# Hybrid decoder block: weight passes in another order, phase arithmetic in other pieces, last scaling by four rows

## The chip, the cores and the metric

The program runs on one core of one Trainium2 chip. The metric is the device time of one execution, in microseconds; the shown time of the kernel before is the median of three runs, 2548.59 us (2547.72 to 2549.03).

## The reference

One layer on 512 tokens of 2048 channels, all in float32. A token mixer has two branches from one projection `w_in` (2048 to 8192 columns): a diagonal state-space branch (64 groups of 64 complex states, a scan over 512 tokens, GELU, a gate `w_glu`, then `w_ssm_out`), and a short gated convolution (three taps, `w_conv_out`). Both are merged by sigmoid gates and go through `w_o`. A gated MLP follows (`w_up` to 2 x 5632, a causal three-tap convolution, GELU, `w_down`), with RMSNorm before each part and at the end:

```python
h = h + token_mixer(rmsnorm(h, norm_tok[l]), w_in[l], a_re[l], a_im[l], log_dt[l], ...)
h = h + conv_ffn(rmsnorm(h, norm_ffn[l]), w_up[l], ffn_conv_w[l], ffn_conv_b[l], w_down[l])
return rmsnorm(h, norm_final)

abar_re = mag * jnp.cos(dt * ai); abar_im = mag * jnp.sin(dt * ai)   # in s5_scan
_, _, xr, xi = lax.associative_scan(combine, (a_seq_re, a_seq_im, bu_re, bu_im), axis=1)
yb = (gate_b * causal_dwconv(gate_c * v, conv_w, conv_b)) @ w_conv_out  # in token_mixer
```

## The kernel before

Channels lie on the 128 partitions and the 512 tokens run along the free axis. Every product with a weight is taken in three passes of rounded numbers: weight and activation are each split into a rounded part (hi) and the remainder (lo), and hi·hi, hi·lo and lo·hi are added up in PSUM. A `Unit` is one output tile of 128 channels; it consists of chunks of eight (in `w_down` six) weight tiles of 128x128, and a chunk of eight is 24 matmuls (`products`, lines 156 to 170).

`run` goes through all chunks in order. After the matmuls of chunk i it calls `after(i)` (line 172), which puts the instructions of the other engines into their queues: first the preparation of chunk i+3 (`prep_to`), then loads, then so many pieces from the list `bg` as the unit says, then the unit's hooks, and at a unit's last chunk its `done`. Each engine works through its own queue in this order, so what is written earlier stands earlier. Three buffers each hold the raw weights (`wraw`), hi (`whi`) and lo (`wlo`).

`prep_to` makes hi by a ScalarE copy (L150). Lo is made in one of two ways. In most of the projection `w_in`, for two chunks of three, ScalarE writes the rounded weight with its sign turned into `wlo` (L145) and then hi (L146), and GpSimd issues a DMA that adds the raw weights onto `wlo` (L147). For all other chunks VectorE subtracts hi from the raw weight (L129).

While TensorE works on `w_in`, the state-space branch runs beside it in `bg` pieces, 32 pairs of groups, three pieces to a pair (`bg_pieces`, line 514). `first` issues the complex rotation of an older pair on GpSimd (`ssm_turn`, six instructions) and half a scan on VectorE; `second` the three ScalarE instructions for sine and cosine (`ssm_trig`) and the other half scan; `third` two small matmuls (`ssm_bu`) and the phase of the next pair (`ssm_phase`: on VectorE the outer sum L449, its rounding by adding and subtracting a large number L451, and the difference L452). One scan half is two products that read PSUM (L98), a sum (L478) and the scan (L479).

The 24 units after the eight of the state-space input are eight triples of the convolution branch: `v_done` copies v out of PSUM and multiplies twice by `rstd` on GpSimd, `gc_done` makes the product with gate c (tile `zp`) and at once the three taps (`conv3`: L610 on ScalarE, L611 and L612 on VectorE) and a product on GpSimd, `gb_done` multiplies by gate b. 32 units of merge gates follow, where one chunk issues one piece, and in every fourth unit two.

The up projection of the MLP (`Pair`) has its own order of passes. The down projection is taken in four blocks; in the last one the final four output tiles are done in two halves of 256 tokens (`ends`), so that the norm of the first half can go on while the second is multiplied. `out_store` (line 1170) scales one row of 128 channels by norm and gain per VectorE instruction and stores two rows at a time.

Of the kernel before, what the change touches and what calls it, by code (L numbers as in the profile page):

```python
# [8 lines left out]
F32 = mybir.dt.float32  # L9
# [7 lines left out]
P = 128  # L17
# [33 lines left out]
class Unit:  # L51
# [7 lines left out]
    def __init__(self, chunks, xs, done, pre=None, bg=0, hooks=None, cols=slice(0, T), late=False, post=None):  # L59
        self.chunks, self.xs, self.done, self.pre, self.bg = chunks, xs, done, pre, bg  # L60
        self.hooks, self.cols, self.late, self.post = hooks or {}, cols, late, post
        self.total = sum(c[1] for c in chunks)
        self.k, self.ps = 0, None
        self.acc, self.off = False, 0


# [1 line left out]
def block_kernel(ctx: ExitStack, tc: tile.TileContext, a: dict):  # L68
# [18 lines left out]

    ones = const.tile([P, P], F32, tag="ones", name="ones")
    nc.vector.memset(ones, 1.0)
    halfpi = const.tile([P, 1], F32, tag="halfpi", name="halfpi")  # L90
    nc.vector.memset(halfpi, math.pi / 2)
    warm = const.tile([P, 1], F32, tag="warm", name="warm")
    nc.scalar.activation(warm, halfpi, AF.Copy)
    rstd = const.tile([P, T], F32, tag="rstd", name="rstd")
# [61 lines left out]
    def products(i, j0, j1):  # L156

        u, c = flat[i]
        if u.ps is None:
            u.ps = psm.tile([P, T], F32, tag="mm", name="mm")  # L160
        base = sum(x[1] for x in u.chunks[:c])
        hi, lo = preps[i]
        for j in range(j0, j1):
            xh, xl = (x[:, u.cols] for x in u.xs(base + j))
            w = slice(j * P, (j + 1) * P)
            first, last = u.k == 0, u.k == u.total - 1
            nc.tensor.matmul(u.ps[:, u.cols], hi[:, w], xh, start=first, stop=False)  # L167
            nc.tensor.matmul(u.ps[:, u.cols], hi[:, w], xl, start=False, stop=False)  # L168
            nc.tensor.matmul(u.ps[:, u.cols], lo[:, w], xh, start=False, stop=last)  # L169
            u.k += 1  # L170

    def after(i):

# [78 lines left out]
    def norm_spread(big, cols=slice(0, T)):  # L252
        pb = psm.tile([P, T], F32, tag="mm", name="statb")
        nc.tensor.matmul(pb[:, cols], ones, big[:, cols], start=True, stop=True)
        return pb
# [18 lines left out]
    def st(tag, bufs=1, shape=(P, T), dt=F32):  # L274
        return sp.tile(list(shape), dt, tag=tag, name=tag, bufs=bufs)
# [164 lines left out]
    def ssm_phase(p):  # L440

        br = braw.pop(p)
        bs = st("bst", 3, (P, 2, P), F32R)
        nc.scalar.activation(bs, br, AF.Copy)
        nc.vector.tensor_tensor(bs[64:], br[64:], bs[64:].bitcast(F32), op=ALU.subtract)
        bst[p] = bs
        ph, nk = st("ph", 2), st("nk")
        ph3 = ph.rearrange("p (a b) -> p a b", a=16)
        nc.vector.tensor_tensor(ph3, pha[:, p, :].unsqueeze(2).to_broadcast([P, 16, 32]),  # L449
                                phb[:, p, :].unsqueeze(1).to_broadcast([P, 16, 32]), op=ALU.add)  # L450
        nc.vector.tensor_scalar(nk, ph, MAGIC, MAGIC, op0=ALU.add, op1=ALU.subtract)  # L451
        nc.vector.tensor_tensor(ph, ph, nk, op=ALU.subtract)  # L452
        phs[p] = ph

    def ssm_trig(p):
        ph = phs.pop(p)
        t = pairt("cs", 3)
        nc.scalar.activation(t[:, 1], ph, AF.Sin, scale=TURN)
        nc.scalar.activation(t[:, 0], ph, AF.Abs)
        nc.scalar.activation(t[:, 0], t[:, 0], AF.Sin, scale=-TURN, bias=halfpi)  # L460
        cs[p] = t

    def ssm_bu(p):
        s_, bs = stacks.pop(p), bst.pop(p)
        w = [ph1ps.tile([P, T], F32, tag=f"w{j}", name=f"w{j}") for j in range(2)]
        for j in range(2):
            nc.tensor.matmul(w[j], bs[:, j, :], s_, start=True, stop=True)
        wri[p] = w
# [14 lines left out]
    def ssm_turn(p):  # L483
        t, z = cs.pop(p), zz.pop(p)
        x = pairt("xx", 5)
        for j in range(2):
            w = st("pt")
            mul(x[:, j], z[:, j], t[:, 0], nc.gpsimd)
            mul(w, z[:, 1 - j], t[:, 1], nc.gpsimd)
            nc.gpsimd.tensor_tensor(x[:, j], x[:, j], w, op=ALU.add if j else ALU.subtract)  # L490
        xx[p] = x
# [22 lines left out]
    def bg_pieces(n):  # L514

        def ok(p):
            return 0 <= p < NPAIR

        def quad(m):
            return m % 4 == 3 and ok(m)  # L520

        def first():
            if quad(n - 6):
                ssm_y((n - 6) // 4)
            if quad(n - 5):
                ssm_out((n - 5) // 4)
            if ok(n - 3):
                ssm_turn(n - 3)
            if ok(n - 2):
                ssm_scan(n - 2, 0)  # L530

        def second():
            if ok(n - 1):
                ssm_trig(n - 1)
            if ok(n - 2):
                ssm_scan(n - 2, 1)

        def third():
            if quad(n - 4):
                ur_load((n - 4) // 4)  # L540
            if ok(n - 1):
                ssm_bu(n - 1)
            if ok(n):
                ssm_phase(n)
                ssm_load(n + 1)
        return [first, second, third]
# [43 lines left out]

    def u_first():
        nc.vector.tensor_copy(rstd, norm_spread(big[0]))
        for i in range(4):
            mul(uts[i], uts[i], rstd)

# [18 lines left out]
    def v_done(i):  # L614
        def f(ps):
            hold["v"] = st("mt", 2)
            nc.scalar.activation(hold["v"], ps, AF.Copy)
            mul(hold["v"], hold["v"], rstd, nc.gpsimd)
            mul(hold["v"], hold["v"], rstd, nc.gpsimd)
        return f  # L620

    def gc_done(i):
        def f(ps):
            z = zpad[i % 2]
            mul(z[:, 2:], ps, hold["v"])
            hold["cv"] = st("cv", 2)
            conv3(hold["cv"], z, "cw", "cb", i, KS)
            mul(hold["cv"], hold["cv"], rstd, nc.gpsimd)
        return f

    def gb_done(i):
        def f(ps):
# [17 lines left out]
    for i in range(8):  # L650
        add(Unit(kd_chunks(w_in, 8 + i), xs1, v_done(i), bg=1),
            Unit(kd_chunks(w_in, 24 + i), xs1, gc_done(i), bg=1),
            Unit(kd_chunks(w_in, 16 + i), xs1, gb_done(i), bg=1))
    merges = [Unit(kd_chunks(w_in, 32 + n), xs1, m_done(n), bg=1 + (n % 4 == 0)) for n in range(2 * KD)]
    add(*merges)
    for u, _ in flat[20:]:
# [496 lines left out]
    def dn_done(i, last, cols=slice(0, T)):  # L1153
        def f(ps):
            h = hrow(i, cols)
            nc.vector.tensor_tensor(h, ps[:, cols], h, op=ALU.add)
            if last:
                sumsq(i, cols)
        return f


# [5 lines left out]
    def out_spread(h):  # L1167
        ff["pb"] = norm_spread(ff["big"], HALVES[h])

    def out_store(h, i0, i1):  # L1170
        cols = HALVES[h]
        for i in range(i0, i1):
            x = hrow(i, cols)
            nc.vector.scalar_tensor_tensor(x, x, V("gf", i), ff["pb"][:, cols], op0=ALU.mult, op1=ALU.mult)
            if i % 2:
                x = ff["H"][i // KS][:, i % KS - 1:i % KS + 1, cols]
                (nc.sync if i % 4 == 1 else nc.scalar).dma_start(
                    out[i - 1:i + 1, :, cols].rearrange("a p t -> p a t"), x)

    for b_, (k0, kn) in enumerate(DOWN):  # L1180
        m = 6 if kn == 12 else 8
        last = k0 + kn == KF

        def down(n, **kw):
            return Unit([(a["w_down"][n][:, k * P:(k + m) * P], m) for k in range(k0, k0 + kn, m)],
                        lambda k, k0=k0: xsd(k0 + k), dn_done(n, last, **kw), late=bool(kw), **kw)

        def shifted(u):
            u.off = SHIFT
            return u  # L1190

        dns = [down(n) for n in range(KD - SPLIT if last else KD)]
        if not last:
            k1, n1 = DOWN[b_ + 1]
            if b_ == 0:
                dns[0].hooks[0] = [lambda: [dg_load(k) for k in range(8, 12)]]
            for j in range(n1):
                dns[3 + j].hooks.setdefault(0, []).append(lambda k=k1 + j: dg_split(k))
        add(*map(shifted, dns))
        if last:  # L1200

            ends = [down(n, cols=c) for c in HALVES for n in range(KD - SPLIT, KD)]
            ends[SPLIT].hooks[0] = [lambda: out_sums(0)]
            ends[SPLIT + 1].hooks[0] = [lambda: out_spread(0)]
            ends[SPLIT + 1].post = lambda: out_store(0, 0, 4)
            ends[SPLIT + 2].post = lambda: out_store(0, 4, 8)
            add(*map(shifted, ends))

    run(3, len(flat))

    out_sums(1)
    out_store(0, 8, KD)
    out_spread(1)
    out_store(1, 0, KD)


# [61 lines left out]
```

## Time and profile before

| what | value |
|---|---|
| median of three runs | 2548.59 us |
| the profiled execution | 2549.99 us, of it 2548.2 us span |
| PE busy | 2497.5 us (98%) |
| DVE, ACT, POOL busy | 1711.2, 1048.8, 559.5 us |
| granted TensorE clock, mean over the span | 0.991 |

The profile is of one execution. Times of instructions are counted from the start of its span. PE is TensorE, PEld its weight loads, DVE is VectorE, ACT is ScalarE, POOL is GpSimd, SP the engine that issues most DMAs. Matmuls overlap one another, so that their durations add up to more than the time they take; the pace is read from counts in a stretch. An idle time is put down to what ended it.

### The profile page before, as it was taken

What the parts mean: (1) busy time and instruction counts of PE and PEld (TensorE: products, weight loads), DVE (VectorE), ACT (ScalarE), POOL (GpSimd) and SP (SyncE); (2) the same over time, 40 slices, a digit from 0 to 9 for tenths busy, and PEclk for the clock granted to TensorE, in tenths of its full rate; (3) what the DMA queues carried; (4) which work ended last, traced back from release to release, by engine and by line L of the source; (5) the groups of instructions that cost most, each with busy time, mean ns of one, the idle gap of its engine ahead of it and who ended that gap; (6) DMA issues with size and microseconds to landing.
All of it is one profiled execution on the core that took longest, in us unless ns stands there. A gap on an engine that the chain in (4) does not pass through costs nothing.

```text
span 2548.2 us, 36443 instructions
## 1 busy us (share of the span) xinstructions
PE 2497.5 (98%) x14616; PEld 2195.8 (86%) x14616; DVE 1711.2 (67%) x1979; ACT 1048.8 (41%) x1331; POOL 559.5 (22%) x431
## 2 busy tenths in 40 slices
PE   8999999999999999999999999999999999999997
PEld 7877777777888888888999999999999988888887
DVE  7799999999323555446777777888787753333335
ACT  5344444444233433334455455555555532222222
POOL 1067767687202121110000000000000000000011
PEclk9999999999999999999999999999999999999999
DMA  5766677777445334444666666676666673434335
GB/s 186 224 165 174 172 187 188 188 190 194 144 147 203 120 132 141 145 142 128 169 174 185 175 167 170 192 190 181 166 177 183 188 254 109 132 108 130 99 94 152
DMA packets 149337, 418.40 MB, mean 164 GB/s; under 512 B 17840, under 2 KB 26160, under 8 KB 149168
## 3 DMA queue, kind: packets, MB, share of 16 engines
q1 hardware_dynamic: 121648, 330.88, 40.8%
q0 software_dynamic: 20448, 74.46, 15.5%
q10 hardware_dynamic: 7072, 10.74, 1.2%
q8 instruction: 114, 1.87, 0.3%
q14 instruction: 55, 0.45, 0.1%
HBM read 300.67 MB, written 40.89 MB: 134 GB/s over the span
## 4 chain that ended last, share of the span: by engine, by line
PE 80%; DMA 5%; DVE 5%; issue 4%; POOL 3%; ACT 2%; SPq 0%; ACTq 0%; DVEq 0%; POOLq 0%
PE mm L169 18%; PE mm L167 18%; PE mm L168 18%; PE sr L1029 9%; PE sr L1027 8%; PE sr L1028 8%; DMA wlo<-wraw 2%; DVE wlo L129 2%; ACT whi L150 1%; DMA wraw<-wraw 1%; POOL pt L98 1%; POOL xx L98 1%; POOL xx L490 1%; PE py L498 1%; DMA th<-ghl 0%
## 5 line engine op out<-in xcount | busy, mean ns | idle before, releaser
L129 DVE TENSOR_TENSOR wlo<-wraw,whi 128x1024 fp32r<-128x1024 f32 (+1 forms) x396 | 479.7, 1211 | 368.8 <-ACT whi L150 368.3
L150 ACT ACTIVATE whi<-wraw 128x1024 fp32r<-128x1024 f32 (+1 forms) x396 | 395.3, 999 | 488.4 <-PE mm L168 391.5
L169 PE MATMUL mm<-xh,wlo 128*128 128x512 f32 x1344 | 530.4, 395 | 23.0 <-DMA wlo<-wraw 20.9
L167 PE MATMUL mm<-xh,whi 128*128 128x512 f32 x1344 | 530.9, 395 | 6.5 <-ACT whi L101 5.7
L168 PE MATMUL mm<-xl,whi 128*128 128x512 f32 x1344 | 528.9, 394 | 0.0
L1029 PE MATMUL sr<-x2h,wlo 128*128 128x256 f32 x1376 | 386.7, 281 | 1.6 <-DVE wlo L129 1.0
L1027 PE MATMUL sr<-x2h,whi 128*128 128x256 f32 x1376 | 384.2, 279 | 0.9 <-ACT whi L150 0.9
L1028 PE MATMUL sr<-x2l,whi 128*128 128x256 f32 x1376 | 383.9, 279 | 0.0
L169 PEld LDWEIGHTS mm<-xh,wlo 128*128 128x128 f32 x1344 | 255.9, 190 | 81.9 <-DMA wlo<-wraw 25.9
L167 PEld LDWEIGHTS mm<-xh,whi 128*128 128x128 f32 x1344 | 255.8, 190 | 67.0 <-issue 6.1
L168 PEld LDWEIGHTS mm<-xl,whi 128*128 128x128 f32 x1344 | 255.8, 190 | 54.7 <-DVE xl L106 0.9
L1029 PEld LDWEIGHTS sr<-x2h,wlo 128*128 128x128 f32 x1376 | 259.7, 189 | 3.9 <-DVE wlo L129 3.4
L1027 PEld LDWEIGHTS sr<-x2h,whi 128*128 128x128 f32 x1376 | 260.1, 189 | 1.1 <-ACT whi L150 1.1
L1028 PEld LDWEIGHTS sr<-x2l,whi 128*128 128x128 f32 x1376 | 260.2, 189 | 0.0
L169 PE MATMUL mm<-x2h,wlo 128*128 128x512 f32 (+1 forms) x528 | 195.4, 370 | 0.8 <-DVE wlo L129 0.8
L167 PE MATMUL mm<-x2h,whi 128*128 128x512 f32 (+1 forms) x528 | 196.1, 371 | 0.0
L168 PE MATMUL mm<-x2l,whi 128*128 128x512 f32 (+1 forms) x528 | 195.2, 370 | 0.0
L1029 PE MATMUL sr<-th,wlo 128*128 128x256 f32 x688 | 192.7, 280 | 1.3 <-DVE wlo L129 1.3
L1027 PE MATMUL sr<-th,whi 128*128 128x256 f32 x688 | 192.4, 280 | 0.0
L1028 PE MATMUL sr<-tl,whi 128*128 128x256 f32 x688 | 192.4, 280 | 0.0
L861 POOL TENSOR_TENSOR acc<-acc,sq 128x512 f32<-128x512 f32 (+1 forms) x31 | 38.5, 1242 | 645.5 <-ACT sq L859 645.5
L129 DVE TENSOR_TENSOR wlo<-r,whi 128x1024 fp32r<-128x1024 f32 x88 | 107.5, 1222 | 47.5 <-ACT whi L150 47.5
(247 smaller groups left out, 4589.2 us busy)
## 6 DMA issues: line engine op xcount, KB each, us to landing
wraw<-in_w_in SPq DMA_DIRECT2D x127, 512.0 KB, 4.3
r<-in_w_up SPq DMA_DIRECT2D x88, 512.0 KB, 6.0
xgb<-in_w_up SPq DMA_DIRECT2D x84, 512.0 KB, 5.3
wraw<-in_w_down SPq DMA_DIRECT2D x104, 384.0 KB, 3.2
wlo<-wraw POOLq DMA_DIRECT2D x56, 512.0 KB, 6.5
wraw<-wraw POOLq DMA_DIRECT2D x43, 512.0 KB, 9.6
wraw<-in_w_o SPq DMA_DIRECT2D x32, 512.0 KB, 3.5
r<-r POOLq DMA_DIRECT2D x22, 512.0 KB, 4.7
```

The source lines that it names most:

```text
L98: eng.tensor_tensor(o, x, y, op=ALU.mult)
L129: nc.vector.tensor_tensor(o, x, y, op=ALU.subtract)
L150: nc.scalar.activation(hi[:, w], raw[:, w], AF.Copy)
L167: nc.tensor.matmul(u.ps[:, u.cols], hi[:, w], xh, start=first, stop=False)
L168: nc.tensor.matmul(u.ps[:, u.cols], hi[:, w], xl, start=False, stop=False)
L169: nc.tensor.matmul(u.ps[:, u.cols], lo[:, w], xh, start=False, stop=last)
L490: nc.gpsimd.tensor_tensor(x[:, j], x[:, j], w, op=ALU.add if j else ALU.subtract)
L498: nc.tensor.matmul(py[32 * q:32 * q + 32, :], cblk[:, p, j, :], xx[p][:, j], start=(j == 0), stop=(j == 1))
L861: nc.gpsimd.tensor_tensor(acc[:, cols], acc[:, cols], ff["sq"][:, cols], op=ALU.add)
L1027: nc.tensor.matmul(ps, hi[:, w], xh, start=(c < 4 and j == 0), stop=False, skip_group_check=c >= 4)
L1028: nc.tensor.matmul(ps, hi[:, w], xl, start=False, stop=False, skip_group_check=c >= 4)
L1029: nc.tensor.matmul(ps, lo[:, w], xh, start=False, stop=j == 7, skip_group_check=c >= 4)
```

## The change

The parts are these.

- `products`: within a chunk, first both passes that use hi for all tiles, then all passes that use lo.
- The state-space phase: the rounding is now a ScalarE instruction (`ssm_round`, adds the large number) in `first`; one VectorE instruction (`ssm_whole`) takes the large number off again and subtracts the phase, in `second`; the three sines move from `second` to `third`, and their sign is turned.
- The convolution branch: `v_done` multiplies once by `acc`, which `u_first` has set to `rstd` squared; the taps and the product behind them move from `gc_done` into a hook of the next unit's first chunk (`branch_conv`).
- The end: in the last block of `w_down` ScalarE multiplies each finished row by its gain; `out_store` multiplies four rows by the norm in one instruction and stores four rows; in the last half four of the rows are done by GpSimd, from a copy of the norm that ScalarE makes; the units of `ends` no longer use weight buffers at an offset of 48 elements.

```diff
@@ products
         for j in range(j0, j1):
             xh, xl = (x[:, u.cols] for x in u.xs(base + j))
             w = slice(j * P, (j + 1) * P)
-            first, last = u.k == 0, u.k == u.total - 1
-            nc.tensor.matmul(u.ps[:, u.cols], hi[:, w], xh, start=first, stop=False)
+            nc.tensor.matmul(u.ps[:, u.cols], hi[:, w], xh, start=base + j == 0, stop=False)
             nc.tensor.matmul(u.ps[:, u.cols], hi[:, w], xl, start=False, stop=False)
-            nc.tensor.matmul(u.ps[:, u.cols], lo[:, w], xh, start=False, stop=last)
-            u.k += 1
+        for j in range(j0, j1):
+            xh = u.xs(base + j)[0][:, u.cols]
+            nc.tensor.matmul(u.ps[:, u.cols], lo[:, j * P:(j + 1) * P], xh, start=False,
+                             stop=base + j == u.total - 1)
@@ ssm_phase
-        nc.vector.tensor_scalar(nk, ph, MAGIC, MAGIC, op0=ALU.add, op1=ALU.subtract)
-        nc.vector.tensor_tensor(ph, ph, nk, op=ALU.subtract)
-        phs[p] = ph
+
+    def ssm_round(p):
+        ph, nk = phs[p]
+        nc.scalar.activation(nk, ph, AF.Identity, bias=magic)
+
+    def ssm_whole(p):
+
+        ph, nk = phs[p]
+        nc.vector.scalar_tensor_tensor(ph, nk, MAGIC, ph, op0=ALU.subtract, op1=ALU.subtract)
@@ bg_pieces
+            if ok(n - 1):
+                ssm_round(n - 1)
             if ok(n - 2):
                 ssm_scan(n - 2, 0)
 
         def second():
             if ok(n - 1):
-                ssm_trig(n - 1)
+                ssm_whole(n - 1)
             if ok(n - 2):
                 ssm_scan(n - 2, 1)
...
             if ok(n - 1):
+                ssm_trig(n - 1)
                 ssm_bu(n - 1)
@@ u_first, v_done, gc_done
         nc.vector.tensor_copy(rstd, norm_spread(big[0]))
+        mul(acc, rstd, rstd)
...
-            mul(hold["v"], hold["v"], rstd, nc.gpsimd)
-            mul(hold["v"], hold["v"], rstd, nc.gpsimd)
+            mul(hold["v"], hold["v"], acc, nc.gpsimd)
...
             mul(z[:, 2:], ps, hold["v"])
-            hold["cv"] = st("cv", 2)
-            conv3(hold["cv"], z, "cw", "cb", i, KS)
-            mul(hold["cv"], hold["cv"], rstd, nc.gpsimd)
         return f
+
+    def branch_conv(i):
+        hold["cv"] = st("cv", 2)
+        conv3(hold["cv"], zpad[i % 2], "cw", "cb", i, KS)
+        mul(hold["cv"], hold["cv"], rstd, nc.gpsimd)
...
-            Unit(kd_chunks(w_in, 16 + i), xs1, gb_done(i), bg=1))
+            Unit(kd_chunks(w_in, 16 + i), xs1, gb_done(i), bg=1, hooks={0: [lambda i=i: branch_conv(i)]}))
@@ dn_done, out_store, ends
             if last:
                 sumsq(i, cols)
+                nc.scalar.activation(h, h, AF.Copy, scale=V("gf", i))
...
-        for i in range(i0, i1):
-            x = hrow(i, cols)
-            nc.vector.scalar_tensor_tensor(x, x, V("gf", i), ff["pb"][:, cols], op0=ALU.mult, op1=ALU.mult)
-            if i % 2:
-                x = ff["H"][i // KS][:, i % KS - 1:i % KS + 1, cols]
-                (nc.sync if i % 4 == 1 else nc.scalar).dma_start(
-                    out[i - 1:i + 1, :, cols].rearrange("a p t -> p a t"), x)
+        for i in range(i0, i1, 4):
+            x = ff["H"][i // KS][:, i % KS:i % KS + 4, cols]
+            r = ff["pb"][:, cols]
+            eng = nc.vector
+            if own and i == KD - 4:
+                eng, r = nc.gpsimd, rstd[:, cols]
+                nc.scalar.activation(r, ff["pb"][:, cols], AF.Copy)
+            eng.tensor_tensor(x, x, r.unsqueeze(1).to_broadcast([P, 4, T // 2]), op=ALU.mult)
+            (nc.scalar if i % 8 else nc.sync).dma_start(out[i:i + 4, :, cols].rearrange("a p t -> p a t"), x)
...
-            add(*map(shifted, ends))
+            add(*ends)
...
-    out_store(1, 0, KD)
+    out_store(1, KD - 4, KD, True)
+    out_store(1, 0, KD - 4)
```

The queues show what that moves. This is ScalarE in one triple of the convolution branch in the kernel before: the first tap (`cv`) stands ahead of two preparations (`wlo`, `whi`; the third, `whi` alone, is of a chunk whose lo VectorE makes), and the sines (`cs`) behind that.

```order
L610 ACTIVATE cv<-zp_104,vec 128x512
L145 ACTIVATE wlo<-wraw 128x1024
L146 ACTIVATE whi<-wraw 128x1024
L444 ACTIVATE bst<-braw 128x256
L145 ACTIVATE wlo<-wraw 128x1024
L146 ACTIVATE whi<-wraw 128x1024
L150 ACTIVATE whi<-wraw 128x1024
L458 ACTIVATE cs<-ph 128x512
L459 ACTIVATE cs<-ph 128x512
L460 ACTIVATE cs<-cs,halfpi 128x512
```

And the same engine and place in the changed kernel (its own line numbers; `nk` is the new rounding):

```order
L147 ACTIVATE wlo<-wraw 128x1024
L148 ACTIVATE whi<-wraw 128x1024
L467 ACTIVATE cs<-ph 128x512
L468 ACTIVATE cs<-ph 128x512
L469 ACTIVATE cs<-cs,consts 128x512
L447 ACTIVATE bst<-braw 128x256
L623 ACTIVATE cv<-zp_105,vec 128x512
L147 ACTIVATE wlo<-wraw 128x1024
L148 ACTIVATE whi<-wraw 128x1024
L457 ACTIVATE nk<-ph,consts 128x512
L152 ACTIVATE whi<-wraw 128x1024
```

The first preparation now stands ahead of the first tap, and the sines stand between a preparation and the small copy `bst` that VectorE waits for.

GpSimd at the same place before: the product behind the taps (`cv`) stands ahead of both DMA issues for lo.

```order
L490 TENSOR_TENSOR xx<-xx,pt 128x512
L98 TENSOR_TENSOR cv<-cv,rstd 128x512
L147 DMA wlo<-wraw 128x1024 x2
L98 TENSOR_TENSOR xx<-zz,cs 128x512
L98 TENSOR_TENSOR pt<-zz,cs 128x512
```

And in the changed kernel:

```order
L499 TENSOR_TENSOR xx<-xx,pt 128x512
L149 DMA wlo<-wraw 128x1024
L100 TENSOR_TENSOR cv<-cv,rstd 128x512
L149 DMA wlo<-wraw 128x1024
L100 TENSOR_TENSOR xx<-zz,cs 128x512
L100 TENSOR_TENSOR pt<-zz,cs 128x512
```

One of the two DMA issues has gone ahead of the product that waits for the taps; the other is still behind it.

VectorE in one pair before:

```order
L445 TENSOR_TENSOR bst<-braw,bst 64x256
L449 TENSOR_TENSOR ph<-pha,phb 128x512
L451 TENSOR_SCALAR nk<-ph 128x512
L452 TENSOR_TENSOR ph<-ph,nk 128x512
L98 TENSOR_TENSOR zz<-w_1549,cs 128x512
L98 TENSOR_TENSOR dt_1614<-w_1550,cs 128x512
```

and in the changed kernel, down to the new instruction L462:

```order
L448 TENSOR_TENSOR bst<-braw,bst 64x256
L452 TENSOR_TENSOR ph<-pha,phb 128x512
L100 TENSOR_TENSOR zz<-w_1549,cs 128x512
L100 TENSOR_TENSOR dt_1612<-w_1550,cs 128x512
L487 TENSOR_TENSOR zz<-zz,dt_1612 128x512
L488 SCALAR_TENSOR_TENSOR zz<-sm_mag,zz 128x512
L131 TENSOR_TENSOR wlo<-wraw,whi 128x1024
L462 SCALAR_TENSOR_TENSOR ph<-nk,ph 128x512
```

Two instructions behind the outer sum are gone, and one stands half a scan later.

## Rows read from the trace of the kernel before

**Rows 1.** Busy times, of the page: time (share of the span) x instructions.
```profile
PE 2497.5 (98%) x14616; PEld 2195.8 (86%) x14616; DVE 1711.2 (67%) x1979; ACT 1048.8 (41%) x1331; POOL 559.5 (22%) x431
```

**Rows 2.** Windows: stretch, length; busy (count) of PE, PEld, DVE, ACT, POOL; clock, DMA, GB/s.
```profile
100.00:600.00 500.00, 476.99 (x2077) 381.18 (x2076) 468.61 (x429) 215.76 (x284) 338.41 (x244) 0.97 0.71 184
700.00:800.00 100.00, 100.00 (x443) 82.81 (x442) 30.78 (x29) 32.38 (x40) 9.93 (x7) 1.00 0.50 169
```

**Rows 3.** A group of PE from 100 to 600: busy us, mean ns | idle before.
```profile
L498 PE MATMUL py<-xx,cblk 128*32 128x512 f32 x96 | 11.5, 598 | 0.0
```

**Rows 4.** Timeline of PE at one such wait: start, length, [idle before, releaser].
```profile
211.00 0.78 PE L169 MATMUL mm<-xh,wlo 128*128 128x512 f32 x1 [2.23 <-DMA wlo<-wraw]
211.58 0.63 PE L167 MATMUL mm<-xh,whi 128*128 128x512 f32 x1
212.01 0.63 PE L168 MATMUL mm<-xl,whi 128*128 128x512 f32 x1
```

**Rows 5.** Waits of PE and ACT from 100 to 600: us in total, times, longest.
```profile
PE mm L169 <- DMA wlo<-wraw: 20.9, 10, 4.4
...
ACT cs L458 <- DVE ph L452: 67.6, 17, 8.8
ACT cv L610 <- DVE zp L98: 60.4, 8, 8.6
```

**Rows 6.** Timeline of all engines ahead of the wait that ends at 423.
```profile
414.25 0.63 ACT L458 ACTIVATE cs<-ph 128x512 f32<-128x512 f32 x1 [8.76 <-DVE ph L452]
...
417.11 1.06 ACT L145 ACTIVATE wlo<-wraw 128x1024 fp32r<-128x1024 f32 x1 [0.46 <-ACT mt L601]
...
418.47 0.89 POOL L147 DMA_DIRECT2D wlo<-wraw  x1 [1.23 <-ACT wlo L145]
...
423.07 0.79 PE L169 MATMUL mm<-xh,wlo 128*128 128x512 f32 x1 [2.83 <-DMA wlo<-wraw]
```

**Rows 7.** Groups of DVE from 100 to 600.
```profile
L452 DVE TENSOR_TENSOR ph<-ph,nk 128x512 f32<-128x512 f32 x29 | 46.2, 1594 | 1.0
L451 DVE TENSOR_SCALAR nk<-ph 128x512 f32<-128x512 f32 x29 | 42.8, 1476 | 1.0
L129 DVE TENSOR_TENSOR wlo<-wraw,whi 128x1024 fp32r<-128x1024 f32 x28 | 41.0, 1464 | 4.7 <-ACT whi L150 4.7
L612 DVE SCALAR_TENSOR_TENSOR cv<-zp,vec,cv 128x512 f32<-128x512 f32 x8 | 8.8, 1097 | 0.3
```

**Rows 8.** Single lines from 100 to 600: duration in ns, shortest/median/longest.
```profile
L479 DVE TENSOR_TENSOR_SCAN zz<-sm_mag,zz x57: 1224/2194/2535, 118.3 to 594.2; 128x512 f32<-128x512 f32 x57
L478 DVE TENSOR_TENSOR zz<-zz,dt x58: 691/693/3882, 117.6 to 599.8; 128x512 f32<-128x512 f32 x58
L452 DVE TENSOR_TENSOR ph<-ph,nk x29: 692/1664/4064, 110.7 to 590.0; 128x512 f32<-128x512 f32 x29
L451 DVE TENSOR_SCALAR nk<-ph x29: 426/1385/4000, 110.2 to 589.5; 128x512 f32<-128x512 f32 x29
L612 DVE SCALAR_TENSOR_TENSOR cv<-zp,vec,cv x8: 752/752/1671, 128.9 to 388.5; 128x512 f32<-128x512 f32 x8
L490 POOL TENSOR_TENSOR xx<-xx,pt x56: 1297/1628/2099, 135.3 to 599.8; 128x512 f32<-128x512 f32 x56
L98 POOL TENSOR_TENSOR mt<-mt,rstd x16: 1298/1492/1742, 110.8 to 374.4; 128x512 f32<-128x512 f32 x16
```

**Rows 9.** The end: DVE timeline; then the DMA view from 2529 to 2549, 40 slices.
```profile
2541.09 3.22 DVE L1174 SCALAR_TENSOR_TENSOR xgb<-xgb,vec,statb 128x256 f32<-128x256 f32 x8
...
GB/s 0 199 311 336 203 0 0 0 0 0 0 0 0 0 0 260 301 340 342 317 340 330 338 344 332 332 338 328 342 328 334 350 320 348 29 0 0 16 0 16
```

**Rows 10.** Groups over the whole span, shapes apart.
```profile
L1029 PE MATMUL sr<-x2h,wlo 128*128 128x256 f32 x1376 | 386.7, 281 | 1.6 <-DVE wlo L129 1.0
...
L981 DVE TENSOR_TENSOR wraw<-r 128x1024 f32<-128x1024 f32 x22 | 26.8, 1219 | 0.0
...
L169 PE MATMUL mm<-x2h,wlo 128*128 128x256 f32 x96 | 27.3, 285 | 0.8 <-DVE wlo L129 0.8
```

More of the change, by code (lines that the diff above doesn't have):

```diff
@@ L62, in __init__ @@
         self.total = sum(c[1] for c in chunks)
-        self.k, self.ps = 0, None
+        self.ps = None
         self.acc, self.off = False, 0
@@ L89, in block_kernel @@
     nc.vector.memset(ones, 1.0)
-    halfpi = const.tile([P, 1], F32, tag="halfpi", name="halfpi")
+    consts = const.tile([P, 2], F32, tag="consts", name="consts")
+    halfpi, magic = consts[:, 0:1], consts[:, 1:2]
     nc.vector.memset(halfpi, math.pi / 2)
+    nc.vector.memset(magic, MAGIC)
     warm = const.tile([P, 1], F32, tag="warm", name="warm")
@@ L446, in ssm_phase @@
         bst[p] = bs
-        ph, nk = st("ph", 2), st("nk")
+        ph, nk = phs[p] = st("ph", 2), st("nk")
         ph3 = ph.rearrange("p (a b) -> p a b", a=16)
@@ L450, in ssm_phase @@
                                 phb[:, p, :].unsqueeze(1).to_broadcast([P, 16, 32]), op=ALU.add)
-        nc.vector.tensor_scalar(nk, ph, MAGIC, MAGIC, op0=ALU.add, op1=ALU.subtract)
-        nc.vector.tensor_tensor(ph, ph, nk, op=ALU.subtract)
-        phs[p] = ph
+    def ssm_round(p):
[4 more added lines that the diff above has]
+        nc.vector.scalar_tensor_tensor(ph, nk, MAGIC, ph, op0=ALU.subtract, op1=ALU.subtract)
     def ssm_trig(p):
-        ph = phs.pop(p)
+        ph, _ = phs.pop(p)
         t = pairt("cs", 3)
-        nc.scalar.activation(t[:, 1], ph, AF.Sin, scale=TURN)
+        nc.scalar.activation(t[:, 1], ph, AF.Sin, scale=-TURN)
         nc.scalar.activation(t[:, 0], ph, AF.Abs)
@@ L1168, in out_spread, with out_store @@
         ff["pb"] = norm_spread(ff["big"], HALVES[h])
-    def out_store(h, i0, i1):
+    def out_store(h, i0, i1, own=False):
         cols = HALVES[h]
-        for i in range(i0, i1):
-            x = hrow(i, cols)
-            nc.vector.scalar_tensor_tensor(x, x, V("gf", i), ff["pb"][:, cols], op0=ALU.mult, op1=ALU.mult)
-            if i % 2:
-                x = ff["H"][i // KS][:, i % KS - 1:i % KS + 1, cols]
-                (nc.sync if i % 4 == 1 else nc.scalar).dma_start(
-                    out[i - 1:i + 1, :, cols].rearrange("a p t -> p a t"), x)
+        for i in range(i0, i1, 4):
[7 more added lines that the diff above has]
+            (nc.scalar if i % 8 else nc.sync).dma_start(out[i:i + 4, :, cols].rearrange("a p t -> p a t"), x)
     for b_, (k0, kn) in enumerate(DOWN):
```

## The prediction

> **What bounds the kernel now.** I read the busy times first: PE is busy for 98% of the span, 2497.5 of 2548.2 us [rows 1], so a gain has to come out of the 51 us in which it is not, or out of time in which it is busy but slow. Then windows, to find where that is. In an undisturbed stretch 443 matmuls of 512 columns pass in 100 us, 0.2257 us each, at granted clock 1.00 [rows 2]. From 100 to 600, where the state-space pieces run beside `w_in`, there are 2077 in 500 us. Of these 96 are the small `py` matmuls with 11.5 us together [rows 3]; the other 1981 need 1981 x 0.2257 = 447.1 us at the undisturbed pace. So 500 - 447.1 - 11.5 = 41.4 us are lost there: 23.0 us idle (500 - 476.99), the remaining 18.4 us slow. The reader sees why it is slow in one wait: PE stops for 2.23 us, and behind that matmuls start 0.43 us apart in place of 0.23 (212.01 follows 211.58) [rows 4]; the granted clock of the 500 us is 0.97 [rows 2], so of 2.4 GHz about 3% is missing, 15 us.
>
> The waits say on what PE stops: 20.9 of the 23.0 us are ten waits of the lo pass for the DMA that completes `wlo`, at most 4.4 us [rows 5]. What makes that DMA late is seen by going back in time from one of them [rows 6]: PE stops until 423.07; the DMA was issued at 418.47, behind the ScalarE copy at 417.11, and ScalarE had stood still for 8.76 us until VectorE was done with the phase (L452). In all ScalarE waits 67.6 us for that phase, and 60.4 us with its first tap for the product `zp` [rows 5]. VectorE is the late one: busy 468.6 of 500 us [rows 2].
>
> **The passes.** A chunk's first lo pass is the third matmul before and the seventeenth after: 14 x 0.2257 = 3.16 us later. Ten waits of 2.1 us on average (20.9/10) and 4.4 us at most would leave one of about 1.2 us, if everything else kept its time. It doesn't: without those waits PE asks for the next chunk sooner, and a later first lo pass gives 3.16 us once, not anew in every chunk. The waits stay away only if VectorE, GpSimd and ScalarE can do a pair's work in the time PE needs. The number of matmuls and weight loads is unchanged, so I count no other cost; at the start, where activations arrive one by one, up to six lo passes now stand behind the last arrival of the first piece: 0 to 6 x 0.43 = 2.6 us at the slow spacing [rows 4], I take 0.6.
>
> **The phase.** VectorE loses L451 and L452, mean 1.476 and 1.594 us, and gains one instruction with two inputs and a constant, for which the nearest row is the tap L612, 1.097 us [rows 7]: 1.97 us a pair, 57 us over the 29 pairs of the stretch. That is one end. The shortest durations of the same lines are 0.426, 0.692 and 0.752 [rows 8], 0.37 us a pair, 10.6 us in all. That is the other end, and the distance between them is waiting inside the instruction: L451 takes 0.43 or 4.00 us for the same work [rows 8]. The Trainium skill, SBUF — State Buffer, section "SBUF: two separate sides", says that VectorE instructions with two SBUF inputs and GpSimd instructions share a pair of ports that one of them holds for a whole instruction while the other is blocked. The spread in rows 8 agrees with that; by the rule the saving would lie at the lower end, since what waited at L451 would wait elsewhere. I let VectorE's load fall to something between 468.6 - 57 = 411 and 468.6 - 10.6 = 458 us, against the 500 - 38 = 462 us that PE would need without idle time and slow clock (23 + 15 = 38). It stays below at both ends, barely at the upper.
>
> ScalarE gains a rounding per pair, about as long as a sine (0.63 us [rows 6]), 18 us in a stretch in which it is busy 215.8 of 500 us [rows 2]; hidden, except that it waits for the outer sum of VectorE with the next preparation behind it. Before, the sine waited there for an instruction further back (L452), so I count no new loss; if VectorE lags as it does now, it is one more wait of the kind of 67.6 us / 17 = 4 us.
>
> **The convolution branch.** Its product drops one GpSimd multiplication, 8 x 1.5 us (median 1.492 [rows 8]), and `u_first` adds one of VectorE (0.7 us, once). The first tap no longer stands ahead of the preparation whose `wlo` PE waits for, so that the 60.4 us of ScalarE waiting [rows 5] move behind it, and GpSimd issues one lo DMA ahead of the product that waits for the taps. The other is still behind. This takes the cause of the waits in the triples away and not just their length.
>
> **Sum for w_in.** 38 us can be had. I expect four fifths, 30 us: the rest is the long wait that 3.16 us don't cover, and a VectorE that stays between 89% (411/462) and 99% (458/462) loaded, where order and jitter still cost some stops with their slow matmuls.
>
> **The end.** Outside w_in the same reordering in the last halves removes 0.8 us of idle time [rows 10]. The 256-column matmuls take 285 ns there with the weight buffers' offset, 281 ns in the up projection without [rows 10]; over 288 of them that is 1.2 us at most, of either sign, I take -0.3. The gain multiplications on ScalarE lie beside the matmuls. In the tail VectorE does 24 single rows, three groups of eight in about 3.14 us each, 0.39 us a row [rows 9], while the stores run at some 335 GB/s for the whole time. 24 rows of 128 KB are 3.15 MB, 9.4 us at that rate, and 24 x 0.39 is also 9.4 us: both end together. Four rows in one instruction are about 1.22 us (1024 columns, L981 [rows 10]); five such are 6.1 us with GpSimd doing the sixth, 3.3 us less, but the stores still need 9.4 us and start after four rows and no longer after two, 0.4 us later. Range -3.3 to +1; I take +0.3, by the rate in rows 9.
>
> -30 - 0.8 - 0.3 + 0.3 + 0.6 = -30.2 us. The profiled execution took 2549.99 us, so 2519.8; it was 1.4 us above the median of 2548.59, so the forecast for the median is 2518.4 us.
>
> **The rivals.**
> A, the forecast: PE is the bound again in the stretch; gain 24 to 41 us, 2508 to 2525.
>
> B: the time that VectorE and GpSimd block each other binds. Take the shortest duration of each instruction that I hold to be exclusive [rows 8]: scan 57 x 1.224, sums 58 x 0.691, L452 and as much for L449 29 x 1.384, L451 29 x 0.426, taps 16 x 0.752, lo 28 x 1.22 (as L981): 209 us; GpSimd 168 x 1.297 for the rotations and 24 x 1.298 for the products: 249 us. Together 458 of 500 us, 92%, while much of the rest is lost to order. The change takes 10.6 + 8 x 1.298 = 21 us off; at the same 92% the stretch lasts 437/0.916 = 477 us, a gain of 23, and with less luck in the order half of it: 2525 to 2537. For it: L451, L452 and the scans spend up to half of their time or more over their shortest [rows 7, 8]. Against: half of that sum is GpSimd's, which is idle for 162 of the 500 us, so 92% is no fixed yield. The Trainium skill's rule on the shared ports, cited above, is this case.
>
> C: the wait only moves. VectorE's rate sets the pace, the instruction saved just waits elsewhere, and only the 3.16 us once are gained: 2545. Against: the work taken from GpSimd and from ScalarE's queue ahead of the preparation.
>
> D, the other side: the sines, now in `third`, end too late. Half a scan of the pair starts one piece later and reads them, and the small copy for `bst`, on which VectorE waits, stands behind them. If VectorE stands still for the three sines, 3 x 0.63 = 1.9 us, in each of 29 pairs, it is 55 us more on 468.6 - 10.6 = 458, so 513 and, with some stops of its own as now, about 525 for what took 500: 2574. It decides from the point where ScalarE is the later of the two. Against: ScalarE waits for VectorE with the sine now, 8.8 us at the longest [rows 5, 6], so VectorE would have to gain that much first.
>
> **How the numbers follow.** A 0.63, B 0.26, C 0.05, D 0.06. What a measurement of this kernel can tell from no change is about 0.2%, 5.1 us, 2543.5 to 2553.7. A and B lie below, C within, D above: faster 0.89, the same 0.05, slower 0.06. The range goes from 2507 (nearly all 38 us and the better tail) to 2537, the far end of B; C, D and a little of A and B, together under 0.2, are outside.
>
> **What would show it.** From 100 to 600 the count of 512-column matmuls per 100 us should come near 440 and PE's idle time fall to a few us; the granted clock back to 1.00. ScalarE's first tap should no longer be a long wait, and VectorE's busy share fall well below 94%. If VectorE stays at 94% and PE waits for lo with fewer but longer stops, B is right; if the instruction ahead of a scan waits for a sine, D. In the tail, stores at an unbroken 335 GB/s with VectorE idle would show the transfer as the bound. It would be wrong if PE's pace of 0.2257 us itself changes with the order of passes, which no row of before can show.

## The result and the profile after

The changed kernel takes 2515.09 us (median of four runs, 2512.01 to 2517.59), the kernel before 2548.15 us in the runs beside it: ratio 0.987, 95% interval 0.9852 to 0.9887. The forecast was 2518.4 us. The profiled execution took 2517.59 us with a span of 2515.6 us, 32.6 us shorter than the span before.

Where the 32.6 us come from is seen in the same window as in [rows 2] (columns as there: busy time and count of PE, PEld, DVE, ACT, POOL, then clock and DMA). This is the changed kernel:

```profile
100.00:600.00 500.00, 494.39 (x2215) 397.25 (x2214) 467.18 (x432) 248.16 (x333) 355.97 (x248) 1.00 0.76 195
```

2215 matmuls now pass where 2077 did. Of the 138 more, 16 are small `py` matmuls (112 in the line below, 96 in [rows 3]), so the gain is 122 x 0.2257 = 27.5 us and 2 us for the 16, 29.5 us in all.

```profile
L507 PE MATMUL py<-xx,cblk 128*32 128x512 f32 x112 | 13.5, 598 | 0.0
```

PE is idle for 5.6 us in place of 23.0, and the granted clock is 1.00 in place of 0.97. DVE is busy as before, 467.2 of 500 us, but it does more pairs in that time (31 in place of 29). What each engine waits for in the same stretch, PE first, then ACT (total, times, longest):

```profile
PE mm L168 <- ACT whi L148: 3.2, 2, 2.2
PE mm L172 <- DMA wlo<-wraw: 2.4, 2, 1.7
```

```profile
ACT wlo L147 <- PE mm L172: 94.1, 20, 8.3
ACT cs L467 <- DVE ph L462: 62.4, 22, 7.7
ACT nk L457 <- DVE ph L452: 41.7, 12, 5.0
...
ACT cv L623 <- DVE zp L100: 4.5, 3, 1.5
```

Against [rows 5], ten waits of PE for the lo DMA (20.9 us) are two (2.4 us). ACT's wait of the first tap for `zp` has gone from 60.4 to 4.5 us. Its waits for the phase have not gone: 67.6 us before, 62.4 + 41.7 now. New at the top is that ACT waits for PE's last lo pass, which releases a `wlo` buffer: the preparation is more often ahead of PE (94.1 us of such waits, 28.3 before).

The phase in VectorE's rows, which answer to [rows 7] (busy us, mean ns | idle before):

```profile
L452 DVE TENSOR_TENSOR ph<-pha,phb 128x512 f32<-128x512 f32 x31 | 49.4, 1593 | 1.0
...
L462 DVE SCALAR_TENSOR_TENSOR ph<-nk,ph 128x512 f32<-128x512 f32 x31 | 40.7, 1314 | 0.0
```

The one instruction that replaced two takes 1.314 us on average, more than the 1.097 us it was priced at. At the end of the span the tail looks like this, first DVE, then the stores in 40 slices from 2496 to 2516:

```profile
2502.43 2.34 DVE L1195 TENSOR_TENSOR xgb<-xgb,statb 128x1024 f32<-128x1024 f32 x2
2505.66 2.35 DVE L1195 TENSOR_TENSOR r<-r,statb 128x1024 f32<-128x1024 f32 x2 [0.89 <-ACT rstd L1194]
2507.93 1.22 DVE L1195 TENSOR_TENSOR xgb<-xgb,statb 128x1024 f32<-128x1024 f32 x1
```

```profile
GB/s 0 0 0 0 252 342 354 100 0 0 0 0 0 0 0 0 0 262 348 328 340 352 344 209 352 315 359 346 268 360 346 348 342 350 340 346 35 0 0 0
```

DVE needs five instructions of 1.2 us for 20 of the 24 rows and is idle for a time in between, but the stores take some 9.5 us for their 3.15 MB, about 330 GB/s on average and mostly near 345, as long as in [rows 9].

The last halves of the down projection, 288 matmuls of 256 columns, have become shorter too: 35.0 us from the first to the end of the last, 37.6 before. Their lo passes, which answer to the last line of [rows 10], in the changed kernel:

```profile
L172 PE MATMUL mm<-x2h,wlo 128*128 128x256 f32 x96 | 13.8, 279 | 0.0
```

So of the 32.6 us, 29.5 lie from 100 to 600 and 2.6 in the last halves; the first 30 us lose about 1.5 (see the last experiment). The other 2 us are spread over the long rest of the span, where the kernels of this document differ by up to 3 us in their single profiles, with the change or without.

### The profile page after: what moved, and what is told of

Read it like the earlier page. It is cut to its first block, busy times and chain, and to the rows that moved or that the text cites. A ratio compares the mean times of both kernels' runs of the same rounds, so it can differ in the third digit from the quotient of the medians.

```text
span 2515.6 us, 36421 instructions
## 1 busy us (share of the span) xinstructions
PE 2482.3 (99%) x14616; PEld 2184.4 (87%) x14616; DVE 1665.4 (66%) x1924; ACT 1079.2 (43%) x1384; POOL 565.4 (22%) x424
## 4 chain that ended last, share of the span: by engine, by line
PE 84%; DVE 7%; DMA 4%; issue 3%; ACT 2%; SPq 0%; DVEq 0%; ACTq 0%; POOLq 0%
PE mm L168 19%; PE mm L169 19%; PE mm L172 19%; PE sr L1043 8%; PE sr L1042 8%; PE sr L1041 8%; DVE wlo L131 2%; DMA wraw<-wraw 2%; ACT whi L152 2%; DVE zz L487 1%; DVE wraw L995 1%; DVE ph L452 0%; PE w L476 0%; DMA braw<-in_b 0%; DMA xgb<-xgb 0%
## 5 line engine op out<-in xcount | busy, mean ns | idle before, releaser
L131 DVE TENSOR_TENSOR wlo<-wraw,whi 128x1024 fp32r<-128x1024 f32 (+1 forms) x396 | 486.0, 1228 | 325.7 <-ACT whi L152 287.1
L168 PE MATMUL mm<-xh,whi 128*128 128x512 f32 x1344 | 527.6, 393 | 10.6 <-ACT whi L103 5.8
L172 PE MATMUL mm<-xh,wlo 128*128 128x512 f32 x1344 | 332.9, 389 | 2.4 <-DMA wlo<-wraw 2.4
L1008 POOL DMA_DIRECT2D wraw<-wraw x43 | 37.0, 861 | 446.8 <-DVE ap L1061 422.2
```

Of the source, the lines that this page charges most:

```text
L131: nc.vector.tensor_tensor(o, x, y, op=ALU.subtract)
L168: nc.tensor.matmul(u.ps[:, u.cols], hi[:, w], xh, start=base + j == 0, stop=False)
L172: nc.tensor.matmul(u.ps[:, u.cols], lo[:, j * P:(j + 1) * P], xh, start=False, stop=base + j == u.total - 1)
L1008: nc.gpsimd.dma_start(gs[G]["s4"], s, accum_op=ALU.add)
```

## The experiments

Two groups of four took the change apart: the changed kernel without one part, and the kernel before with one or two parts. Four more kernels followed, for questions that these left open. All were timed in five rounds beside the kernel before, the second group on another chip. The kernel before took 2545.1 to 2548.2 us in these sets, so kernels of different sets are compared by the ratio rather than by the median. The texts put on record ahead of each run name theories: SLACK and LOAD, and ORDER, which was made after the first group.

| kernel | median us | ratio to before | 95% interval |
|---|---|---|---|
| changed kernel | 2515.09 | 0.9870 | 0.9852 to 0.9887 |
| without the pass order | 2523.42 | 0.9906 | 0.9891 to 0.9921 |
| without the phase | 2514.25 | 0.9871 | 0.9857 to 0.9886 |
| without the branch | 2524.61 | 0.9912 | 0.9897 to 0.9926 |
| without the end | 2515.73 | 0.9880 | 0.9864 to 0.9897 |
| pass order alone | 2534.45 | 0.9954 | 0.9942 to 0.9967 |
| branch alone | 2523.73 | 0.9914 | 0.9899 to 0.9929 |
| phase alone | 2535.88 | 0.9962 | 0.9949 to 0.9974 |
| pass order and branch | 2514.28 | 0.9879 | 0.9865 to 0.9892 |
| taps moved, alone | 2527.03 | 0.9920 | 0.9904 to 0.9936 |
| extra product, an input from PSUM | 2519.63 | 0.9899 | 0.9881 to 0.9916 |
| extra product, both inputs in SBUF | 2543.55 | 0.9989 | 0.9979 to 0.9998 |
| start and earlier stores | 2510.30 | 0.9854 | 0.9834 to 0.9874 |

**Without the pass order.** Hi, hi and lo of a tile stand together again:

```diff
             nc.tensor.matmul(u.ps[:, u.cols], hi[:, w], xl, start=False, stop=False)
-        for j in range(j0, j1):
-            xh = u.xs(base + j)[0][:, u.cols]
-            nc.tensor.matmul(u.ps[:, u.cols], lo[:, j * P:(j + 1) * P], xh, start=False, ...)
+            nc.tensor.matmul(u.ps[:, u.cols], lo[:, w], xh, start=False, ...)
```

> The changed kernel, but each weight tile's three passes stand together again (hi, hi, lo); all else changed. Theory SLACK (the 3.16 us of later lo passes cover the waits): most of the gain is lost, 2535 to 2545 us, and PE waits for lo as before, some 20 us from 100 to 600. Theory LOAD (work taken off VectorE, GpSimd and ScalarE's queue is what counts): most of the gain stays, 2515 to 2522 us, PE waits under 8 us.

Measured 2523.42 us, between the two theories and much nearer LOAD: PE waits 10.9 us for lo. The windows of this kernel say where:

```profile
100.00:390.00 290.00, 290.00 (x1300) 235.73 (x1300) 264.13 (x262) 141.75 (x188) 204.69 (x142) 1.00 0.76 193
390.00:600.00 210.00, 199.15 (x885) 156.98 (x884) 194.71 (x170) 103.70 (x142) 152.13 (x106) 0.98 0.75 192
```

In the triples (100 to 390) PE isn't idle at all, without any slack for lo. All 10.9 us of waits are among the merge units. The pass order is worth about 8 us on top of the rest (9 by the ratios); from 100 to 600 all of it lies there.

**Without the phase.** The old functions `ssm_phase` and `ssm_trig`, no `ssm_round` and `ssm_whole`, the sines in `second`.

> The changed kernel with the old phase: rounding and difference as two VectorE instructions, sines in the second piece. SLACK: the time stays within 4 us of 2515, since waits up to 3.2 us are covered. LOAD: VectorE is late again, 2525 to 2538 us, and ScalarE waits some 60 us for the phase from 100 to 600.

Measured 2514.25 us, as the changed kernel. ACT's sines wait longer for the phase than in the kernel before (67.6 us) or the changed one (62.4, and 41.7 for the rounding), and PE does not notice (100 to 600; then PE from 30 to 720):

```profile
ACT cs L461 <- DVE ph L455: 87.4, 17, 9.7
```

```profile
PE mm L172 <- DVE wlo L131: 1.8, 2, 1.0
PE mm L168 <- ACT whi L148: 1.3, 1, 1.3
PE mm L172 <- DMA wlo<-wraw: 1.1, 1, 1.1
```

So VectorE's saved work and the moved sines add nothing that could be measured to the other parts. As the last part to be put in, the phase is worth nothing, which SLACK had and LOAD had not.

**Without the branch.** `v_done` with two products, taps in `gc_done`, no `branch_conv`.

> The changed kernel with the old convolution branch: two GpSimd products with rstd, taps at once behind gate c. SLACK: within 4 us of 2515. LOAD: the waits of the triples come back, about 12 us from 100 to 390, 2522 to 2530 us, with ScalarE's first tap waiting some 50 us for zp.

Measured 2524.61 us. ACT's first tap waits 92.1 us, and the clean stretch of the triples is gone, in spite of pass order and phase (first ACT, then the window):

```profile
ACT cv L622 <- DVE zp L100: 92.1, 8, 12.1
```

```profile
100.00:390.00 290.00, 285.26 (x1270) 229.36 (x1269) 256.89 (x245) 132.24 (x177) 212.49 (x144) 1.00 0.72 183
```

1270 matmuls stand against 1302 in the changed kernel, where PE isn't idle in this stretch: 7.2 us. The time is as LOAD put it, but PE's idle time in the triples is 4.7 us and not 12, and ACT's wait 92 and not 50. VectorE has the saved phase here and the waits are back all the same, so its saved work is not what takes them away. The reading is that an instruction that waits stands ahead of a preparation; the run with the taps moved alone, below, tests it.

**Without the end.** `out_store` by single rows, stores of two rows, offset buffers in `ends`.

> The changed kernel with the old end: single rows scaled by VectorE, stores of two rows, weight buffers of the last units at their offset. By the forecast the end is worth about nothing (-3.3 to +2 us): 2514 to 2517 us, with VectorE's 24 rows and the stores ending together. If single rows were the bound of the tail, 2518 us or more.

Measured 2515.73 us; the intervals of the two kernels overlap, so the times tell no gain of the end, as forecast. The profiles tell 1.2 us: with the old end the 288 matmuls of the last halves take 36.3 us (so in all three kernels with the new pass order and the offset), with the new one 35.0 (in five kernels with the new order). VectorE's 24 rows are back in three groups like this one, and the tail lasts as long (16.9 us from the last weight matmul, 16.8 in the changed kernel).

```profile
2505.26 3.21 DVE L1188 SCALAR_TENSOR_TENSOR xgb<-xgb,vec,statb 128x256 f32<-128x256 f32 x8
```

**Pass order alone.**

> The kernel before with only the pass order changed. ORDER (what counts is how late lo may come and what stands ahead of a preparation in ScalarE's and GpSimd's queues; VectorE's saved instructions are worth nothing): about 2525 us, as the changed kernel without its branch part (2524.6). LOAD (VectorE's rate decides): the waits come back, 2535 us or more.

Measured 2534.45 us: not the 2525 us of ORDER, and half a microsecond under LOAD's bound. The waits of PE for lo (30 to 720) are shorter, and a new kind appears:

```profile
PE mm L170 <- DMA wlo<-wraw: 8.6, 7, 1.7
PE mm L166 <- ACT whi L146: 7.5, 6, 3.3
PE mm L170 <- DVE wlo L129: 2.5, 3, 1.0
```

Lo may come 3.16 us later, but hi may not, and ACT makes hi behind the same waits: 68.1 us for `zp` and 118.6 us for the phase in this kernel. When lo stops being the last to arrive, hi is. PE's idle time from 100 to 600 falls only from 23.0 to 17.6 us, but 61 more matmuls pass, 13.8 us. The rest of these is pace, at a granted clock of 1.00 in place of 0.97:

```profile
100.00:600.00 500.00, 482.37 (x2138) 384.48 (x2137) 475.63 (x440) 217.50 (x288) 343.93 (x248) 1.00 0.74 188
```

**Branch alone.**

> The kernel before with only the convolution branch changed (one product with rstd squared, taps one chunk later). ORDER: about 2524 us, as the changed kernel without its pass order (2523.4), no waits in the triples (100 to 390), those among the merge units left. LOAD: GpSimd loses 12 us and VectorE nothing: 2535 us or more.

Measured 2523.73 us, as ORDER had it; two thirds of the whole gain come from this part alone. PE is idle for 0.9 us in the triples, and 9.7 us among the merge units:

```profile
100.00:390.00 290.00, 289.12 (x1294) 234.43 (x1293) 276.52 (x274) 128.51 (x167) 202.58 (x143) 1.00 0.77 192
390.00:600.00 210.00, 200.26 (x896) 157.79 (x895) 203.36 (x183) 96.19 (x129) 150.23 (x107) 0.99 0.76 193
```

**Taps moved, alone.** The branch part without the product with `rstd` squared.

> The kernel before with only the taps moved one chunk later; GpSimd keeps both products with rstd. ORDER: nearly all of what the branch part alone gave, 2524 to 2528 us, as ScalarE's first tap no longer holds up the preparation. If the saved GpSimd product were the main thing: 2535 us or more.

Measured 2527.03 us, ratio 0.9920 against 0.9914 with the product: the intervals overlap nearly whole. It is the place of the taps, and of the product behind them, that counts; the saved product may hold a small share (PE is idle for 3.0 us in the triples here, 0.9 with the product saved).

Two queues are changed by that move, and no run parts them. In the kernel before, five of the six waits of the triples look like this one (ACT, then GpSimd, then PE):

```profile
127.23 0.82 ACT L610 ACTIVATE cv<-zp,vec 128x512 f32<-128x512 f32 x1 [8.61 <-DVE zp L98]
127.95 1.05 ACT L145 ACTIVATE wlo<-wraw 128x1024 fp32r<-128x1024 f32 x1
129.71 1.29 POOL L98 TENSOR_TENSOR cv<-cv,rstd 128x512 f32<-128x512 f32 x1 [14.54 <-DVE cv L612]
130.95 1.77 POOL L147 DMA_DIRECT2D wlo<-wraw  x2
135.64 0.55 PE L169 MATMUL mm<-xh,wlo 128*128 128x512 f32 x1 [2.46 <-DMA wlo<-wraw]
```

ScalarE begins the copy for lo only behind the tap, after 8.61 us of waiting. The copy ends at 129.0, but GpSimd issues the DMA at 130.95, behind its own product: 1.95 us more, nearly the whole of PE's 2.46. The text on record speaks of ScalarE's tap alone; GpSimd's product stands in the way as well.

**Phase alone.**

> The kernel before with only the phase changed. ORDER: 2544 to 2549 us, since ScalarE still waits for zp with the preparation behind it, and PE waits some 18 us for lo from 100 to 600. LOAD: VectorE is 10 to 57 us less loaded, 2525 to 2538 us.

Measured 2535.88 us: 8 us faster than ORDER had it and within the range of LOAD. By itself the phase is worth some 9.7 us (0.0038 of 2546). PE still waits for lo (30 to 720), with ACT's first tap 70.5 us behind `zp`:

```profile
PE mm L171 <- DMA wlo<-wraw: 18.9, 11, 2.7
```

The waits are about as many as before and shorter: at most 2.7 us in place of 4.4. ACT waits 52.2 us for the phase (31.1 with the sines and 21.1 with the rounding) in place of 67.6, but longer for `zp`, 70.5 in place of 60.4. Whether the 9.7 us come from VectorE's saved work or from the new places of sines and rounding in ScalarE's queue isn't shown: the run changes both. That nothing of it is left once the taps are out of the way is shown by the sums (phase, branch and end together, in the kernel without the pass order, 0.9906, against 0.9914 for the branch alone); why, no row shows.

**Pass order and branch.**

> The kernel before with pass order and branch together, old phase, old end. ORDER: 2513 to 2516 us, all of the gain. LOAD: 2520 us or more, as the phase is missing.

Measured 2514.28 us: all of the gain with two of the four parts. PE's idle time in the triples is zero and 3.8 us among the merge units.

**Extra work for VectorE.** Two kernels put 64 more products into the changed kernel, one per half scan, whose result nothing reads:

```diff
         mul(t, wri[p][1 - j], s)
+        mul(st("ul", 1, (P, T), F32R).bitcast(F32), wri[p][j], c)      # or cs[p][:, 1] for wri[p][j]
```

> The changed kernel with one more VectorE product per half scan, 64 in all, that nothing reads and that takes one input from PSUM, about 0.68 us each, 44 us in all. If VectorE has reserve, as ORDER says, under half of that shows: 2518 to 2537 us. If VectorE were the bound, 2555 us.

> The same with both inputs in SBUF: the same work, and 0.69 us alone. PORT (VectorE with two SBUF inputs and GpSimd block each other for whole instructions): the extra instruction takes 1.2 to 2 us on average and the kernel is 8 us or more slower than the one with an input from PSUM. NO PORT: the same time within 4 us, 0.7 us per instruction.

Measured 2519.63 and 2543.55 us. The rows of the extra instruction, from PSUM and from SBUF, first 100 to 600, then all 64 with shortest, median and longest duration in ns:

```profile
L100 DVE TENSOR_TENSOR ul<-w,cs 128x512 f32<-128x512 f32 x61 | 41.2, 676 | 0.0
...
L100 DVE TENSOR_TENSOR ul<-w,cs x64: 672/675/682, 115.6 to 619.3; 128x512 f32<-128x512 f32 x64
```

```profile
L100 DVE TENSOR_TENSOR ul<-cs 128x512 f32<-128x512 f32 x57 | 59.2, 1039 | 0.0
...
L100 DVE TENSOR_TENSOR ul<-cs x64: 672/678/3589, 117.1 to 645.4; 128x512 f32<-128x512 f32 x64
```

and PE's waits in the latter (30 to 720):

```profile
PE mm L172 <- DMA wlo<-wraw: 10.2, 10, 2.2
PE w L476 <- DVE bst L448: 7.9, 3, 3.6
```

43 us more of work that reads PSUM (64 x 0.676) cost 4.5 us of time by the medians and 7.4 by the ratios. The same work with both inputs in SBUF takes 68.6 us and costs 23.9 us more than that. The mean of 1.2 to 2 us was too high for the extra instruction (1.07 over all 64), but the kernel is more than 8 us slower, as PORT had it.

That GpSimd is the reason can be read from starts and ends in the trace. With both inputs in SBUF, 23 of the 64 meet no GpSimd instruction, and they take 0.672 to 0.682 us; the 41 that do meet one take 1.293 us on average and up to 3.589. With an input from PSUM, 47 meet a GpSimd instruction, and none takes longer than 0.682. The Trainium skill, SBUF — State Buffer, section "SBUF: two separate sides", says that a VectorE instruction with two SBUF inputs and a GpSimd instruction that reads SBUF share a pair of ports, which whichever starts first holds for its whole length. The trace agrees.

The price in time is another matter. The extra instructions are 25.3 us longer in sum, and the kernel 23.9 us: nearly all of it shows, where of the first 43 us little did. VectorE was by then busy for 492.2 of the 500 us (467.2 in the changed kernel):

```profile
100.00:600.00 500.00, 491.49 (x2200) 394.37 (x2199) 492.16 (x483) 243.75 (x329) 353.32 (x247) 1.00 0.74 192
```

So the reserve that ORDER speaks of is there, and it is about used up by the first 43 us; beyond it VectorE's load does decide.

**Start and earlier stores.** In the changed kernel, the first three calls of `products` keep the three passes of a tile together, and the first half's last eight rows are stored ahead of the last sums:

```diff
-            ends[SPLIT + 1].post = lambda: out_store(0, 0, 4)
-            ends[SPLIT + 2].post = lambda: out_store(0, 4, 8)
+            ends[SPLIT + 1].post = lambda: out_store(0, 0, 8)
+            ends[SPLIT + 2].post = lambda: out_store(0, 8, KD)
...
-    out_store(0, 8, KD)
```

> The changed kernel with two edits. In the first three pieces, before all activations are there, the three passes of a tile stand together: 1 to 1.5 us. The first half's rows 8 to 15 are scaled and stored ahead of the last sums, so that 2 MB and no longer 3 MB are stored behind the last matmul; if the transfer at some 340 GB/s bounds the tail that is 3.1 us. Together 2510 to 2512 us. If VectorE or the norm bounds the tail, 2514 us.

Measured 2510.30 us (2508.05 to 2512.51), the fastest median of all; its interval overlaps with that of the changed kernel, so the two places are judged by the profile. From 0 to 30 PE passes 91 instructions; the changed kernel 81 (second fence):

```profile
0.00:30.00 30.00, 23.51 (x91) 17.59 (x92) 19.44 (x29) 22.03 (x29) 2.13 (x5) 1.00 0.83 303
```

```profile
0.00:30.00 30.00, 22.57 (x81) 16.52 (x82) 18.41 (x28) 20.82 (x28) 0.20 (x4) 1.00 0.78 288
```

Ten instructions are some 2.3 us, but single profiles differ here: the eight kernels with the new pass order at the start have 81 to 89 in this stretch, 85.3 on average, and the six with the three passes together 88 to 93, 90.5 on average. Five instructions, some 1.2 us, are what the start is worth by all of them. The stores from 2490 to 2510 now stand in three pieces, the last 6.5 us long in place of 9.5:

```profile
GB/s 340 340 348 342 98 0 0 0 0 70 350 309 361 348 348 307 4 0 0 0 0 0 0 0 0 190 346 326 348 350 272 352 344 348 344 352 342 277 2 0
```

From the last weight matmul's end to the end of the span it is 15.5 us (2495.02 to 2510.49), in the changed kernel 16.8 us: 1.4 of the 3.1 us. The rest went into a longer wait: VectorE's first scaling instruction of the second half stood still until ScalarE had copied the norm for GpSimd. In the changed kernel rows of the first half filled that time, and the same wait was 0.89 us.

```profile
2500.55 2.35 DVE L1197 TENSOR_TENSOR r<-r,statb 128x1024 f32<-128x1024 f32 x2 [1.79 <-ACT rstd L1196]
```

## Why the prediction was right, and which of its steps was not

**Where and how much.** That nearly all of the gain lies from 100 to 600 held: 29.5 us came there, 30 were forecast. Idle time and slow clock went together, as the first part put it: 17.4 of the 29.5 us are idle time, the rest is pace. The closeness of the two numbers is partly luck. The four fifths of 38 us were argued from VectorE's load, and that load turned out not to set the gain; the part that gave the most had no term of its own.

**The passes.** That 3.16 us alone would not do, since the waits come back if nothing else changes, held in part: alone the pass order gave 0.46% of the 1.30%. That is 11.7 us, though, and not 3.16 "once", so the step that a later lo pass doesn't help anew in every chunk is not borne out. And the reason given for the waits that stay was the rate of the engines. What the run showed is that hi, which got no slack, became the late one (7.5 us of waits that the kernel before didn't have).

**The phase.** This step failed. The forecast took VectorE's lower load as the condition of the gain and expected its busy share "well below 94%"; it is 93.4% (467.2 of 500 us). The saving itself is real and within the range of 10.6 to 57 us, which was for 29 pairs: from 30 to 720, which holds all 32 pairs, VectorE is busy 16.0 us less than in the kernel without the phase (568.7 against 584.7), and 38.7 us less with the phase alone than in the kernel before (550.9 against 589.6). But it isn't the condition: without the phase the kernel is as fast, and with 43 us of further work only 4.5 to 7.4 us slower. Alone on the kernel before the phase gave 9.7 us, so it is not worthless; it works on the waits that the branch part removes too. That PE notices VectorE's lateness only where an instruction waiting for it stands ahead of a weight preparation fits all of these runs, and is argued from them.

**The branch.** The mechanism was named, "the cause of the waits in the triples", and no size was given to it. It is the largest part: 0.86% alone, of 1.3%. That the saved GpSimd product matters little was not foreseen and not needed. The prediction told both queues, ScalarE's and GpSimd's, and how much each is worth stays open.

**The end and the start.** The tail was forecast at +0.3 us and came out at -0.2 (17.0 us from the last weight matmul to the end before, 16.8 after): VectorE's rows are done sooner and the stores last as long, which is, but for two slices at 209 and 268 GB/s, the sign that was named for the transfer as the bound. The last halves were forecast at -0.8 - 0.3 and came out at -2.6: 1.3 with the pass order alone and 1.2 more with the end. The start was taken at 0.6 of up to 2.6 us; this profile has seven PE instructions fewer in the first 30 us than the one before, 1.6 us, and all profiles together give some 1.2.

**The rivals.** B, the shared ports as the bound, was the nearest: that VectorE and GpSimd hold each other up is shown by the two extra products, but the change leaves enough room that it doesn't decide. Its sign, fewer but longer stops at 94%, came in part: VectorE stays at 93.4%, and PE's stops for lo are fewer (two for ten) but shorter (1.7 us at most for 4.4). The rule as the prediction put it, two inputs in SBUF, doesn't cover L451, which has one and yet spreads from 0.426 to 4.000 us [rows 8]. C did not come for the change as a whole. D did not come in the time, but its second way has rows: VectorE waits longer for the small copy `bst`, which now stands behind the sines (100 to 600; first before, then the changed kernel), and 27.2 us with the phase alone.

```profile
DVE bst L445 <- ACT bst L444: 8.2, 7, 3.4
...
DVE bst L448 <- ACT bst L447: 13.8, 9, 3.4
```

## What to carry to other kernels

Look for an instruction that waits on a slow engine and stands, in an in-order queue, ahead of the work that feeds the bound engine; moving two such instructions, in two queues, behind that work gave six tenths of this gain (0.80 of 1.30%). Taking load off the slow engine gave something by itself (0.38%) and nothing on top, as long as that engine had reserve. When one operand gets slack, ask whether the other one is made behind the same wait. Parts that gain on the same wait do not add up, so each is priced both alone and as the one left out: alone they give 0.46, 0.38 and 0.86%, together with the end 1.30%.

## What was not expected of the hardware

A product of VectorE with one input from PSUM keeps its 0.676 us beside a busy GpSimd: 47 of 64 met a GpSimd instruction, and none took longer than 0.682. The same product with two inputs in SBUF takes 0.682 us at most where it meets none, and 1.293 us on average where it does. 64 of the first cost 4.5 to 7.4 us of time; 64 of the second cost 23.9 us more, in a kernel in which VectorE had no reserve left.
